# A hybrid attention and PEER layer on one core: one or two gathers used behind each of the last 20 tiles ahead of the first up product, and the second low part of these tiles on VectorE

## The chip, the core and the metric

The kernel runs on one core of a Trainium2 chip. Its engines are TensorE (PE, matmuls), VectorE (DVE), ScalarE (ACT), GpSimd (POOL) and SyncE (SP, which here only issues transfers); each works through its own row of instructions in order, and waits at an instruction until what it needs is there. Transfers run on 16 DMA engines. The metric is the time of one execution in microseconds (us) on the device, the median of several runs.

## What is computed

The reference is one layer: attention with two groups of heads, an output projection, and then PEER, a layer of 16,384 experts of one neuron each, of which every token chooses 128 (8 heads, 16 each). There are 512 tokens of width 2048, in float32. The change lies within PEER:

```
def peer(x, w_query, sub_keys, expert_down, expert_up):
    q = (xt @ w_query).reshape(T, PEER_HEADS, 2, PEER_HALF)
    scores = jnp.einsum('thpc,hpnc->thpn', q, sub_keys).astype(jnp.float32)
    vals, idx = lax.top_k(scores, PEER_TOPK)
...
    experts = (i1 * PEER_N_KEYS + i2).reshape(T, PEER_HEADS * PEER_TOPK)
    gates = jax.nn.softmax(top_vals, axis=-1)...
    def block(args):
        xc, ec, gc = args
        u = jnp.take(expert_down, ec, axis=0)
        hdn = jax.nn.gelu(jnp.einsum('ted,td->te', u, xc))
        vsel = jnp.take(expert_up, ec, axis=0)
        return jnp.einsum('te,ted->td', gc * hdn, vsel)
```

## The kernel before

PEER is computed in two ways at once. For the first 320 tokens the kernel multiplies with all experts: 128 **down tiles** (one for each 128 experts; 128 x 320 numbers come out, and GELU puts them into `hold`), a product with a dense table of gates, and **up products** that add into `yacc`. For the other 192 tokens it fetches only the chosen experts' rows: 384 **gather steps**. A step (`gather_step`) issues one indirect transfer on POOL's queue (128 rows of 2048 floats, one for each partition, into one of four buffers `rows`) and one **use** of them on DVE (L517 for the down table, which is a dot product, L525 for the up table, which adds into `yg`). The steps are part e (64 tokens twice, 64 steps down and 64 up), then part g (128 tokens, 128 and 128). At the end of part e its result is finished and written, and part g's row of inputs is loaded.

Matmuls are in a float32 form that takes two parts of each operand: `hi`, made by ACT from the loaded `raw`, and `lo`, the difference, made by DVE or POOL; three matmuls (L99 to L101) stand for one. A down tile consists of two pieces ("halves", 24 matmuls each); `down_tile(e, lo_on)` gives the engine that makes `lo` for each. There are two buffers of `hi` and two of `lo`, three of `raw`. An up product for one of 16 columns c has 24 matmuls and parts `uhi` and `ulo`, made by ACT and DVE from `uraw`.

The order in the program:
- the gates stage, in which the dense table of gates is made and written to memory (`o` comparisons on DVE, L680 and L681), with 40 gather steps;
- 38 down tiles ahead of the first up product: 28 whose `hold` is written to memory for later, and 10 that stay. I number them 0 to 37. Before the change POOL makes both low parts of tiles 0 to 27; of tiles 28 to 37 POOL makes the first and DVE the second, and one gather step stands behind each;
- the main loop, 16 groups g of 16 columns c. At the start of a group its eight `hold` are split into `hn` parts (L801 on ACT, L802 on DVE). For the first 180 columns there is one down tile (both low parts on DVE) for every two columns, for the last 76 there is none; `due` counts the gather steps behind each column.

A scheduler decides where on each engine the instructions stand, from the order of the program and its own costs; a gather step's use is only tied to stand behind the matmul that it was given. So several tiles of the 38 stand among the gates stage's instructions: the trace has tiles 19 to 37 behind it.

```
        for e in range(NE1 - SPILL, NE1):
            down_tile(e, (G, G))
            DMA.dma_start(hid_d[e - (NE1 - SPILL)], hold[e])
        for e in range(HOLD):
            mm = down_tile(e, (G, V))
            gather_step(mm)
```

## Time and profile before

| | |
|---|---|
| median of 3 runs | 3319.63 us (3317.11 to 3323.86) |
| profiled execution: its time, its span | 3313.15 us, 3311.4 us |
| TensorE busy | 3098.8 us, 94% of the span |
| DVE busy | 2497.5 us, 75% |
| POOL busy | 967.6 us, 29% |
| granted TensorE clock, mean | 0.976 of full speed |
| transfers | 846.50 MB, mean 256 GB/s |

The span runs from the first instruction to the last of the profiled execution. A share of busy time is a mean over stages with different limits: what a change in one stage is worth is read from that stage.

### The profile page before, as it was taken

The numbers are of one execution on the slowest core, as the hardware profiler recorded it, in microseconds if no ns is written. First come the engines' busy times: TensorE is split into PE (matmuls) and PEld (weight loads), VectorE is DVE, ScalarE is ACT, GpSimd is POOL, SyncE is SP. The second block draws the span as 40 slices with busy tenths as digits, with TensorE's granted clock in tenths as the row PEclk, the third lists the DMA queues.
The fourth block names the chain that finished last, engine by engine and source line by source line (L and its number), as shares of the span: only waits on it lengthen the run. The fifth ranks groups of instructions, "written<-read, shape, count | busy, mean of one in ns | idle before, by whom it ended". The sixth has DMA issues, their size and how long they took to land.

```text
span 3311.4 us, 47208 instructions
## 1 busy us (share of the span) xinstructions
PE 3098.8 (94%) x18265; PEld 2828.8 (85%) x18265; DVE 2497.5 (75%) x3724; ACT 1214.8 (37%) x1863; POOL 967.6 (29%) x529
## 2 busy tenths in 40 slices
PE   6999999999998877889999999999999999998987
PEld 4887778878876667778999999999999999998877
DVE  5225665454357899992799998998999999988885
ACT  4224444343231117884333333332333333322233
POOL 2000000000024445766434433333433344432210
PEclk9999999999999889999999999999999999999999
DMA  4322222214432136887799999999999999999983
GB/s 178 98 94 75 69 69 73 70 62 137 130 128 71 64 116 239 323 331 266 278 391 388 394 397 365 396 402 359 378 404 392 397 396 404 374 377 366 349 307 117
DMA packets 215792, 846.50 MB, mean 256 GB/s; under 512 B 20944, under 2 KB 69456, under 8 KB 163216
## 3 DMA queue, kind: packets, MB, share of 16 engines
q1 hardware_dynamic: 159424, 439.37, 37.1%
q0 software_dynamic: 55296, 402.68, 30.5%
q8 instruction: 143, 2.34, 0.3%
q10 hardware_dynamic: 848, 1.44, 0.1%
q14 instruction: 81, 0.66, 0.1%
HBM read 806.31 MB, written 35.91 MB: 254 GB/s over the span
## 4 chain that ended last, share of the span: by engine, by line
PE 42%; DVE 11%; issue 5%; DMA 3%; POOL 2%; ACT 0%; SPq 0%; ACTq 0%; DVEq 0%; POOLq 0%
PE up L99 7%; PE up L100 7%; PE up L101 7%; PE dn L99 7%; PE dn L100 7%; PE dn L101 6%; DVE o L680 2%; DMA uraw<-in_up_t 2%; DVE o L681 2%; DVE rows L517 2%; DVE ulo L810 1%; DVE yg_g L525 1%; POOL rows L511 1%; POOL lo L94 1%; DVE hn L802 1%
## 5 line engine op out<-in xcount | busy, mean ns | idle before, releaser
L93 ACT ACTIVATE hi<-raw 128x1024 fp32r<-128x1024 f32 x416 | 439.8, 1058 | 733.1 <-PE dn L101 221.9
L99 PE MATMUL up<-hn,ulo 128*128 128x320 f32 x2048 | 646.6, 316 | 55.6 <-DVE ulo L810 55.1
L99 PE MATMUL dn<-hn,lo 128*128 128x320 f32 x2048 | 650.3, 318 | 44.3 <-POOL lo L94 41.8
L94 DVE TENSOR_TENSOR lo<-raw,hi 128x1024 fp32r<-128x1024 f32 x320 | 390.1, 1226 | 352.9 <-ACT hi L93 351.9
L100 PE MATMUL dn<-hn,hi 128*128 128x320 f32 x2048 | 647.2, 316 | 0.0
L101 PE MATMUL dn<-hn,hi 128*128 128x320 f32 x2048 | 645.6, 315 | 0.0
L100 PE MATMUL up<-hn,uhi 128*128 128x320 f32 x2048 | 640.3, 313 | 0.9 <-DVE hn L802 0.9
L101 PE MATMUL up<-hn,uhi 128*128 128x320 f32 x2048 | 639.6, 312 | 0.0
L809 ACT ACTIVATE uhi<-uraw 128x1024 fp32r<-128x1024 f32 x256 | 271.7, 1061 | 648.8 <-PE up L101 504.5
L99 PEld LDWEIGHTS up<-hn,ulo 128*128 128x128 f32 x2048 | 390.9, 191 | 70.4 <-DVE ulo L810 66.0
L99 PEld LDWEIGHTS dn<-hn,lo 128*128 128x128 f32 x2048 | 388.9, 190 | 54.1 <-POOL lo L94 50.5
L100 PEld LDWEIGHTS up<-hn,uhi 128*128 128x128 f32 x2048 | 391.2, 191 | 1.2 <-DVE hn L802 1.2
L101 PEld LDWEIGHTS up<-hn,uhi 128*128 128x128 f32 x2048 | 390.9, 191 | 0.0
L100 PEld LDWEIGHTS dn<-hn,hi 128*128 128x128 f32 x2048 | 389.2, 190 | 0.0
L101 PEld LDWEIGHTS dn<-hn,hi 128*128 128x128 f32 x2048 | 388.8, 190 | 0.0
L810 DVE TENSOR_TENSOR ulo<-uraw,uhi 128x1024 fp32r<-128x1024 f32 x256 | 309.3, 1224 | 49.4 <-PE dn L99 28.6
L511 POOL DMA_INDIRECT rows<-in_up,gidx x128 | 222.9, 1741 | 401.9 <-DVE yg_g L525 380.1
L511 POOL DMA_INDIRECT rows<-in_down,gidx x128 | 209.5, 1637 | 379.1 <-DVE rows L517 347.2
L94 POOL TENSOR_TENSOR lo<-raw,hi 128x1024 fp32r<-128x1024 f32 x96 | 246.3, 2571 | 209.2 <-ACT hi L93 209.0
L525 DVE SCALAR_TENSOR_TENSOR yg_g<-rows,coef_g,yg_g 128x2048 f32<-128x2048 f32 x127 | 298.0, 2347 | 0.0
L517 DVE SCALAR_TENSOR_TENSOR rows<-rows,hng_g 128x2048 f32<-128x2048 f32 x128 | 290.7, 2286 | 3.9 <-DMA rows<-in_down,gidx 2.3
L99 PE MATMUL mm<-xn,lo 128*128 128x512 f32 x512 | 204.5, 399 | 0.0
(259 smaller groups left out, 5003.3 us busy)
## 6 DMA issues: line engine op xcount, KB each, us to landing
raw<-in_down_t SPq DMA_DIRECT2D x256, 512.0 KB
uraw<-in_up_t SPq DMA_DIRECT2D x256, 512.0 KB
raw<-in_w_qk SPq DMA_DIRECT2D x64, 512.0 KB
g_d<-stg SPq DMA_DIRECT2D x10, 2048.0 KB
gt<-g_d SPq DMA_DIRECT2D x32, 640.0 KB
raw<-in_w_v SPq DMA_DIRECT2D x32, 512.0 KB
raw<-in_w_o SPq DMA_DIRECT2D x32, 512.0 KB
raw<-in_w_pq SPq DMA_DIRECT2D x32, 512.0 KB
```

What stands on the lines that cost most here:

```text
L93: A.activation(hi, raw, AF.Copy)
L94: (lo_on or V).tensor_tensor(lo, raw, hi.bitcast(F32), ALU.subtract)
L99: PE.matmul(ps, a[1], b[0], start=first, stop=False)
L100: PE.matmul(ps, a[0], b[1], start=False, stop=False)
L101: return PE.matmul(ps, a[0], b[0], start=False, stop=last)
L511: ld = G.indirect_dma_start(out=rows, out_offset=None, in_=table, in_offset=bass.IndirectOffsetOnAxis(ap=ix[:, j:j + 1], axis=0))
L517: use = V.scalar_tensor_tensor(rows, rows, 1.0, hng[part], ALU.mult, ALU.mult, accum_out=dots[part][:, j:j + 1])
L525: use = V.scalar_tensor_tensor(yg[part], rows, coef[part][:, j:j + 1], yg[part], ALU.mult, ALU.add)
L680: V.tensor_tensor(o2, iob, col(i2t), ALU.is_equal)
L681: V.tensor_tensor(o1, iob, col(i1t), ALU.is_equal)
L809: A.activation(uh, raw, AF.Copy)
L810: V.tensor_tensor(ul, raw, uh.bitcast(F32), ALU.subtract)
```

## The change

Of the 38 tiles ahead of the first up product, the last 20 (numbers 18 to 37) now have their second low part made by DVE, and one gather step behind each, two behind every second one: 30 steps instead of 10. Tiles 28 to 37 had DVE's low part before, so ten low parts move from POOL to DVE. The main loop issues 1.5 steps for a column instead of 1.6 while there are down tiles, and 0.75 instead of 0.8 behind them, since 314 steps are left for it instead of 334.

```diff
+FREE = 18
...
-        for e in range(NE1 - SPILL, NE1):
-            down_tile(e, (G, G))
-            DMA.dma_start(hid_d[e - (NE1 - SPILL)], hold[e])
-        for e in range(HOLD):
-            mm = down_tile(e, (G, V))
-            gather_step(mm)
+        for n, e in enumerate((*range(NE1 - SPILL, NE1), *range(HOLD))):
+            mm = down_tile(e, (G, V if n >= FREE else G))
+            if e >= NE1 - SPILL:
+                DMA.dma_start(hid_d[e - (NE1 - SPILL)], hold[e])
+            for _ in range((n >= FREE) + (n >= FREE and n % 2)):
+                gather_step(mm)
...
-                due += 1.6 if e < NE1 - SPILL else 0.8
+                due += 1.5 if e < NE1 - SPILL else 0.75
                 while due >= 1:
                     gather_step(mm)
                     due -= 1
```

The new constant moves every later line number by one. DVE's row from the end of the gates stage on, before (L517 are uses, L810 is a low part of the first up products, L94 a low part of a down tile):

```order
L681 TENSOR_TENSOR o_10432<-iota_e,i1t 128x1024
L517 SCALAR_TENSOR_TENSOR rows_10428,dots_e<-rows_10428,hng_e 128x2048
L517 SCALAR_TENSOR_TENSOR rows_10455,dots_e<-rows_10455,hng_e 128x2048
L810 TENSOR_TENSOR ulo<-uraw,uhi 128x1024 x2
L94 TENSOR_TENSOR lo<-raw,hi 128x1024
L517 SCALAR_TENSOR_TENSOR rows_12328,dots_e<-rows_12328,hng_e 128x2048
L94 TENSOR_TENSOR lo<-raw,hi 128x1024
```

The same place with the change (L518 are uses, L95 low parts of down tiles, L811 of up products):

```order
L682 TENSOR_TENSOR o_10432<-iota_e,i1t 128x1024
L95 TENSOR_TENSOR lo<-raw,hi 128x1024
L518 SCALAR_TENSOR_TENSOR rows_10428,dots_e<-rows_10428,hng_e 128x2048
L518 SCALAR_TENSOR_TENSOR rows_10455,dots_e<-rows_10455,hng_e 128x2048
L518 SCALAR_TENSOR_TENSOR rows_11689,dots_e<-rows_11689,hng_e 128x2048
L95 TENSOR_TENSOR lo<-raw,hi 128x1024
L518 SCALAR_TENSOR_TENSOR rows_11756,dots_e<-rows_11756,hng_e 128x2048
L518 SCALAR_TENSOR_TENSOR rows_11759,dots_e<-rows_11759,hng_e 128x2048
L95 TENSOR_TENSOR lo<-raw,hi 128x1024
L518 SCALAR_TENSOR_TENSOR rows_11826,dots_e<-rows_11826,hng_e 128x2048
L811 TENSOR_TENSOR ulo<-uraw,uhi 128x1024
L95 TENSOR_TENSOR lo<-raw,hi 128x1024
```

DVE had nothing of tiles 19 to 27 before; now a low part of each stands there, with one or two uses ahead of it, and the first two `ulo` stand among the tiles 20 to 22.

DVE's row in tiles 28 to 37, before (L789 is the product with the gates, L802 a `hn`):

```order
L94 TENSOR_TENSOR lo<-raw,hi 128x1024
L789 TENSOR_TENSOR hold_12392<-hold_12392,gt_12925 128x320
L802 TENSOR_TENSOR hn_6789<-hold_12392,hn_6788 128x320
L517 SCALAR_TENSOR_TENSOR rows_12460,dots_e<-rows_12460,hng_e 128x2048
L94 TENSOR_TENSOR lo<-raw,hi 128x1024
```

With the change:

```order
L95 TENSOR_TENSOR lo<-raw,hi 128x1024
L790 TENSOR_TENSOR hold_12371<-hold_12371,gt_12988 128x320
L803 TENSOR_TENSOR hn_6789<-hold_12371,hn_6788 128x320
L518 SCALAR_TENSOR_TENSOR rows_12439,dots_e<-rows_12439,hng_e 128x2048
L518 SCALAR_TENSOR_TENSOR rows_12442,dots_e<-rows_12442,hng_e 128x2048
L95 TENSOR_TENSOR lo<-raw,hi 128x1024
L790 TENSOR_TENSOR hold_12437<-hold_12437,gt_12988 128x320
L803 TENSOR_TENSOR hn_6789<-hold_12437,hn_6788 128x320
L518 SCALAR_TENSOR_TENSOR rows_12508,dots_e<-rows_12508,hng_e 128x2048
L95 TENSOR_TENSOR lo<-raw,hi 128x1024
```

Every second tile has two uses between `hn` and the next tile's low part. POOL's row has, in all 20 tiles, one low part and then one or two transfers of `rows`.

DVE's row at the seam between groups 4 and 5 of the main loop, before (L817 adds an up product into `yacc`; the last but one and the last of group 4 are here):

```order
L517 SCALAR_TENSOR_TENSOR rows_18481,dots_g<-rows_18481,hng_g 128x2048
L817 TENSOR_TENSOR yacc<-yacc,up 128x320
L517 SCALAR_TENSOR_TENSOR rows_18580,dots_g<-rows_18580,hng_g 128x2048
L517 SCALAR_TENSOR_TENSOR rows_18583,dots_g<-rows_18583,hng_g 128x2048
L802 TENSOR_TENSOR hn_6789<-hold_17455,hn_6788 128x320
L802 TENSOR_TENSOR hn_6789<-hold_17611,hn_6788 128x320
L802 TENSOR_TENSOR hn_6789<-hold_17750,hn_6788 128x320
L802 TENSOR_TENSOR hn_6789<-hold_17887,hn_6788 128x320
L802 TENSOR_TENSOR hn_6789<-hold_18024,hn_6788 128x320
L802 TENSOR_TENSOR hn_6789<-hold_18161,hn_6788 128x320
L802 TENSOR_TENSOR hn_6789<-hold_18303,hn_6788 128x320
L810 TENSOR_TENSOR ulo<-uraw,uhi 128x1024 x2
```

With the change:

```order
L818 TENSOR_TENSOR yacc<-yacc,up 128x320
L803 TENSOR_TENSOR hn_6789<-hold_17497,hn_6788 128x320
L803 TENSOR_TENSOR hn_6789<-hold_17650,hn_6788 128x320
L803 TENSOR_TENSOR hn_6789<-hold_17789,hn_6788 128x320
L818 TENSOR_TENSOR yacc<-yacc,up 128x320
L518 SCALAR_TENSOR_TENSOR rows_18616,dots_g<-rows_18616,hng_g 128x2048
L518 SCALAR_TENSOR_TENSOR rows_18619,dots_g<-rows_18619,hng_g 128x2048
L803 TENSOR_TENSOR hn_6789<-hold_17926,hn_6788 128x320
L803 TENSOR_TENSOR hn_6789<-hold_18063,hn_6788 128x320
L803 TENSOR_TENSOR hn_6789<-hold_18200,hn_6788 128x320
L803 TENSOR_TENSOR hn_6789<-hold_18339,hn_6788 128x320
L811 TENSOR_TENSOR ulo<-uraw,uhi 128x1024 x2
```

Three of the seven `hn` stand ahead of the last `yacc` now. The seams of before differ in the number of uses behind the last `yacc` (one or two) and in how many `hn` stand ahead of it (none to three); with the change five seams are as this one, and six have one use behind the last `yacc`, with two `hn` and the other use between the last two `yacc` and five `hn` behind.

## Rows read from the trace of the kernel before

**Rows 1.** Windows: stretch, its length, busy us (instructions) by engine, granted clock, DMA share, GB/s.

```profile
1500.00:1550.00 50.00, 46.28 (x302) 44.34 (x303) 7.75 (x7) 21.72 (x31) 29.74 (x13) 1.00 0.89 300
1700.00:2000.00 300.00, 298.70 (x2021) 297.90 (x2020) 283.14 (x243) 104.62 (x130) 119.92 (x65) 1.00 1.00 392
2960.00:3200.00 240.00, 207.44 (x1304) 198.49 (x1304) 203.32 (x204) 66.23 (x79) 57.73 (x42) 0.94 0.93 346
```

**Rows 2.** Timeline of ACT, the `hold` of down tiles: start us, us, instruction, idle before.

```profile
1548.84 0.44 ACT L643 ACTIVATE hold<-dn 128x320 f32<-128x320 f32 x1 [3.08 <-PE dn L101]
1556.59 0.44 ACT L643 ACTIVATE hold<-dn 128x320 f32<-128x320 f32 x1 [3.08 <-PE dn L101]
...
1639.59 0.44 ACT L643 ACTIVATE hold<-dn 128x320 f32<-128x320 f32 x1 [2.24 <-PE dn L101]
1647.08 0.44 ACT L643 ACTIVATE hold<-dn 128x320 f32<-128x320 f32 x1 [2.22 <-PE dn L101]
...
1668.73 0.44 ACT L643 ACTIVATE hold<-dn 128x320 f32<-128x320 f32 x1 [2.50 <-PE dn L101]
1682.89 0.44 ACT L643 ACTIVATE hold<-dn 128x320 f32<-128x320 f32 x1 [2.50 <-PE dn L101]
...
2959.73 0.44 ACT L643 ACTIVATE hold<-dn 128x320 f32<-128x320 f32 x1 [6.06 <-PE dn L101]
```

**Rows 3.** The same view, at gaps longer than 14.16.

```profile
1996.19 0.44 ACT L643 ACTIVATE hold<-dn 128x320 f32<-128x320 f32 x1 [2.50 <-PE dn L101]
...
2050.71 0.44 ACT L643 ACTIVATE hold<-dn 128x320 f32<-128x320 f32 x1 [2.50 <-PE dn L101]
...
2121.51 0.44 ACT L643 ACTIVATE hold<-dn 128x320 f32<-128x320 f32 x1 [2.13 <-issue]
2136.59 0.44 ACT L643 ACTIVATE hold<-dn 128x320 f32<-128x320 f32 x1 [2.50 <-PE dn L101]
...
2235.70 0.44 ACT L643 ACTIVATE hold<-dn 128x320 f32<-128x320 f32 x1 [2.50 <-PE dn L101]
2253.86 0.44 ACT L643 ACTIVATE hold<-dn 128x320 f32<-128x320 f32 x1 [2.50 <-PE dn L101]
...
2310.50 0.44 ACT L643 ACTIVATE hold<-dn 128x320 f32<-128x320 f32 x1 [2.50 <-PE dn L101]
2329.25 0.44 ACT L643 ACTIVATE hold<-dn 128x320 f32<-128x320 f32 x1 [2.50 <-PE dn L101]
...
2699.90 0.44 ACT L643 ACTIVATE hold<-dn 128x320 f32<-128x320 f32 x1 [2.49 <-PE dn L101]
2714.45 0.44 ACT L643 ACTIVATE hold<-dn 128x320 f32<-128x320 f32 x1 [2.50 <-PE dn L101]
```

**Rows 4.** Timeline of DVE in tiles 29 and 30.

```profile
1588.39 1.23 DVE L94 TENSOR_TENSOR lo<-raw,hi 128x1024 fp32r<-128x1024 f32 x1 [3.68 <-ACT hi L93]
...
1592.43 2.42 DVE L802 TENSOR_TENSOR hn<-hold,hn 128x320 fp32r<-128x320 f32 x1 [2.41 <-ACT hn L801]
1594.77 2.28 DVE L517 SCALAR_TENSOR_TENSOR rows<-rows,hng_e 128x2048 f32<-128x2048 f32 x1
...
1596.98 1.22 DVE L94 TENSOR_TENSOR lo<-raw,hi 128x1024 fp32r<-128x1024 f32 x1
1598.12 0.48 DVE L789 TENSOR_TENSOR hold<-hold,gt 128x320 f32<-128x320 f32 x1
```

**Rows 5.** Timeline of DVE at the seam of groups 4 and 5.

```profile
2233.75 2.92 DVE L802 TENSOR_TENSOR hn<-hold,hn 128x320 fp32r<-128x320 f32 x7
```

**Rows 6.** Timelines of POOL and DVE in the gates stage.

```profile
1386.15 2.80 POOL L94 TENSOR_TENSOR lo<-raw,hi 128x1024 fp32r<-128x1024 f32 x1 [4.24 <-ACT hi L93]
...
1386.64 4.46 DVE L517 SCALAR_TENSOR_TENSOR rows<-rows,hng_e 128x2048 f32<-128x2048 f32 x1
```

**Rows 7.** Timeline of POOL, the first low part of tile 30.

```profile
1592.12 2.38 POOL L94 TENSOR_TENSOR lo<-raw,hi 128x1024 fp32r<-128x1024 f32 x1 [4.03 <-ACT hi L93]
```

**Rows 8.** DMA queues in the window 1505 to 1655: all transfers.

```profile
DMA packets 14430, 39.78 MB, mean 265 GB/s; under 512 B 1092, under 2 KB 7492, under 8 KB 12968
```

## The prediction

> **What bounds the kernel now.** I read the stretches first, then the gaps between tiles, then single instructions. Four stretches matter: the gates stage up to 1505 us; the last 20 tiles ahead of the first up product (1505 to 1655, "the free stretch"); the up products with a down tile for every two of them (1655 to 2960, "the paired stretch"); the up products alone (2960 to 3295). In the windows [rows 1] the reader is to see that DVE is nearly idle at the start of the free stretch (7.75 of 50 us), that TensorE is full in the paired stretch (298.7 of 300 us, granted clock 1.00) with DVE at 283.1 and the transfers at a share of 1.00 and 392 GB/s, and that in the last stretch neither is full (PE 207, DVE 203 of 240).
>
> The starts of `hold` on ScalarE give the time of every tile [rows 2]. A tile takes 7.75 us where POOL makes both low parts, 7.49 where DVE makes the second, and 14.16 with its two up products. The last is TensorE's own pace: 96 matmuls in 14.16 us, so half a tile (24 matmuls) is 3.54 us and a tile alone would be 7.08. From 1668.73 to 2959.73 there are 89 such gaps; 89 x 14.16 is 1260.2 of 1291.0 us. So the paired stretch loses 30.8 us in all, and only that can be won there, however much DVE work leaves it. Three gaps from 1996.19 to 2050.71 lose 12.0 (the end of part e), the one at 2310.50 loses 4.6 in the middle of a group, and ten of the eleven seams between groups share the other 14.2, and the eleventh lies within the end of part e [rows 3].
>
> **The main loop: 20 uses leave it.** A use costs DVE 2.21 us (1594.77 to 1596.98) [rows 4]. 288 uses in the paired stretch become 270: 18 x 2.21 is 40 us of DVE time, but its price is what TensorE stops waiting. At a seam TensorE has one down tile, 7.08 us, between the last product of a group and the first of the next, and in that time DVE must finish what stands between that product's `yacc` and the next `ulo`. Before, at the seam of 2235.70, these are two uses and seven `hn` (2.92 us in all [rows 5]): 0.4 for `yacc` (of the size of one `hn`), 4.4, 2.9 and 1.14 for `ulo` are 8.8, 1.7 too late, and the gap is 18.16, 4.0 lost, more than the lateness alone. The fractions of 1.6 repeat every five groups, so a second seam is like it. With 1.5 all seams are alike but for where three `hn` go: five have two uses and four `hn` there (0.4 + 4.4 + 1.7 + 1.14 = 7.6, half a us late), six have one use and five `hn` (0.4 + 2.2 + 2.1 + 1.14 = 5.8, in time). Before has one seam of each kind: 2121.51 lost 0.92, 2699.90 lost 0.39 [rows 3]. So 5 x 0.92 + 6 x 0.39 = 6.9 in place of the 14.2: **-7.3**. The lost 4.6 at 2310.50 came with four uses in front of a `ulo`; that order is gone from the middle of groups, but a late `raw` helped to make it: -4.6 at best, 0 at worst, **-2.5** taken. The end of part e issues the same instructions in the middle of a group: **0**, give or take 4. The paired stretch: **-10**, between -16 and -3.
>
> **The up products alone.** 46 uses become 44, so at most 2 x 2.21 = 4.4 us less DVE work where DVE often ends last; but the last use falls one product later, nearer to the closing work of part g: **-2**, between -4.4 and +3.
>
> **The free stretch: 20 uses and 10 low parts arrive.** DVE has the room by its busy time: a pair of tiles (one with one use, one with two) asks 3 x 2.21 + 2 x 1.14 = 8.9 us of 15. What speaks against it is that DVE and POOL don't work at once here. In the gates stage a use that met POOL's `lo` took 4.46 us instead of 2.28, and that `lo` took 2.80 instead of 2.38, since it began behind a running comparison [rows 6]. In the last ten tiles every `hn` takes 2.42 us behind a `lo` of 2.38 that began 0.31 earlier [rows 4, 7]. So to DVE's time POOL's `lo` must be added, and what counts is who comes first.
>
> Tiles 18 to 27. I count from the start of the second `lo` on DVE (1588.39), which takes 1.14; then the uses stand, the first from +1.1 to +3.35, the second to +5.56. POOL wants its `lo` for the next tile at +3.73 (1592.12). In a tile with one use DVE is done at +3.35 and nothing meets. In one with two, the second use starts 0.4 us ahead of POOL, which waits from 3.73 to 5.56, 1.83 us (that it waits behind a use I take from its wait behind a comparison, the nearest row), and TensorE, which in these tiles waits for that `lo` already, waits with it. A pair costs 7.49 + 7.49 + 1.83 = 16.8 us instead of 2 x 7.75 = 15.5: +1.3, five pairs, +6.5. Without that wait the ten tiles would gain 10 x 0.26 = 2.6, which is the lower bound.
>
> Tiles 28 to 37, counted from the end of POOL's `lo` (1594.50). Now `hn` ends at +0.27, a use at +2.48 and the second `lo` is ready at +3.6, just when TensorE has done its first half. With two uses `lo` starts at +4.69 and ends at +5.83; POOL's next `lo`, wanted at +5.12, stands behind it until 8.2. TensorE's second half runs from 5.83 to about 9.4, and an ordinary tile of 7.49 follows: 16.9 a pair instead of 14.98, +1.9, five pairs, **+9.5**. The lower bound is 0, if DVE catches up in the tile with one use. The free stretch: **+16**, between -3 and +24 (8 us of late transfers on top, next).
>
> The Trainium skill, "SBUF — State Buffer", section "Who interferes with whom", has a rule for this: a DVE instruction that reads two inputs from SBUF and a GpSimd instruction that reads SBUF exclude each other, and the one issued second waits for the whole of the first. That the use waits is in these traces (4.46 for 2.28); that POOL's `lo` waits behind a running use, which is the whole of the +6.5, no row shows, only the wait behind a comparison. By the rule it does, and the sum stands; by the shown rows alone the ten tiles could give 2.6 back and the sum would be 9 lower, -5.
>
> **Transfers.** A gather is 128 rows of 2048 floats, 1.05 MB. The free stretch moved 39.8 MB [rows 8]; 20 more make 60.8 MB in 150 us, 405 GB/s, more than the 392 at which the paired stretch is saturated. At 392 it needs 155 us, and about 5 more for its start, where a share of 0.89 moved only 300 GB/s [rows 1]. If the stretch becomes 166 us long by the port, the transfers fit, and hide; early lumps can make a `raw` or the first two `uraw` late, whose `ulo` now stand in DVE's row among the first tiles. No price in the sum, up to +8 in the range.
>
> **Sum.** On the profiled execution (span 3311.4, time 3313.15): +16 - 10 - 2 = **+4**. The median of the runs shown is 6.5 us above that execution, so I put the sum on the median: 3319.6 + 4 = **3323.6 us**. A measurement of this kernel can tell about 0.2%, 6.6 us, from no change; the forecast lies inside that.
>
> **Rivals.**
> 1. Faster: the exclusion costs little. DVE lies idle for stretches of each tile now, and if its row and POOL's `lo` slip past each other, tiles 18 to 27 give 2.6 and the others stay at 7.49; then -3 - 10 - 2 = -15, **3305 us**. For it: the port's own load in a pair of tiles 28 to 37 is 3 x 2.21 + 2 x (1.14 + 0.8 + 2.38) = 15.3 us (0.8 for `hn` and the gate product), hardly over 14.98. Against it: both rows are fixed orders with TensorE between them, and the walk above finds no other place for the second use. It decides where the ten pairs cost under 0.7 us each.
> 2. Slower: the port's +16 and the lumps of transfers at 1505 to 1540 together, with the paired stretch giving only its two bad seams: +22 - 6 + 0 = +16, **3336 us**. It decides where the free stretch grows beyond about 18 us; the 405 GB/s speak for it, the four `rows` buffers filled beforehand (4 x 1.05 MB, 10 us of transfers) against.
> 3. The moved work does nothing, since TensorE is at its pace in 14.16 either way and the free stretch has room: 0 to -3, **3318 us**. The seam of 2235.70 speaks against the first half.
>
> **Chances.** The forecast (+4, from -3 to +10) 0.37; rival 1 0.27; rival 2 0.26; rival 3 0.10. Faster by over 0.2%: rival 1 nearly whole, 0.27. Slower: rival 2 with the upper part of the forecast, 0.36. Within: 0.37. The range takes rival 1 from its middle and rival 2 to its middle: 3305 to 3336.
>
> **What would show it.** Right: tile gaps in the free stretch that alternate between about 7.5 and 9.3, with POOL's `lo` behind a use and DVE's `lo` behind two; seams of the paired stretch all at 14.5 to 15.1, no gap over 15.2 but for the end of part e, and a sum of losses of about 20 in place of 30.8. Wrong: gaps of 7.5 throughout the free stretch (rival 1), or gaps over 10 that end with a `raw`, a `uraw` or `rows` transfer (rival 2); or seams that still lose 4. The likeliest fault is the size of the wait at the port, since it hangs on 0.4 us between the second use and POOL's `lo`.

## The result, and the profile after

The change makes the kernel slower: 3340.47 us in the median (3333.16 to 3344.35) against 3318.37 (3315.39 to 3324.82) for the kernel before, run beside it; the ratio is 1.0063, 95% interval 1.0048 to 1.0077. The profiled execution took 3341.1 us with a span of 3339.3. That is 27.9 us over the profiled span of before, 5.8 more than the medians differ, since the execution profiled before lies below its median. The stages below are compared span against span, one profiled execution of each kernel.

Cut by the starts of `hold`, the 27.9 us arise in three places:

| stretch, by `hold` | before | after | difference | forecast |
|---|---|---|---|---|
| up to tile 18 | 1508.40 | 1508.38 | 0.0 | 0 |
| tiles 18 to 22 | 32.70 | 47.43 | +14.7 | |
| tiles 22 to 37 | 113.48 | 127.27 | +13.8 | |
| free stretch, both together | 146.18 | 174.70 | +28.5 | +16 |
| tile 37 to the last down tile | 1305.15 | 1295.82 | -9.3 | -10 |
| from there to the end | 351.67 | 360.40 | +8.7 | -2 |

Windows of the changed kernel, with columns as in [rows 1]; the last one starts 20 us later than there, since the stretch does:

```profile
1500.00:1550.00 50.00, 36.54 (x216) 35.23 (x215) 24.61 (x21) 16.86 (x26) 21.45 (x11) 0.86 0.95 348
...
1700.00:2000.00 300.00, 291.17 (x1935) 287.48 (x1934) 271.25 (x237) 101.93 (x126) 109.60 (x62) 0.98 0.99 376
2980.00:3220.00 240.00, 203.07 (x1265) 196.70 (x1263) 192.95 (x195) 63.50 (x76) 49.46 (x38) 0.92 0.89 324
```

In the first 50 us TensorE works 36.5 us where it worked 46.3, and the transfers carry 348 GB/s where they carried 300. In the last window DVE works 10 us less than before, the transfers are less full, and yet TensorE does less: something waits there that is neither engine's total.

**The hole behind tile 19.** ACT's timeline, from the `hold` of tile 19 to that of tile 20 and on:

```profile
1516.65 0.44 ACT L644 ACTIVATE hold<-dn 128x320 f32<-128x320 f32 x1 [2.45 <-PE dn L102]
1521.13 1.06 ACT L94 ACTIVATE hi<-raw 128x1024 fp32r<-128x1024 f32 x1 [4.04 <-DMA raw<-in_down_t]
1523.64 1.06 ACT L94 ACTIVATE hi<-raw 128x1024 fp32r<-128x1024 f32 x1 [1.46 <-DMA raw<-in_down_t]
1538.32 1.06 ACT L810 ACTIVATE uhi<-uraw 128x1024 fp32r<-128x1024 f32 x1 [13.62 <-DMA uraw<-in_up_t]
1539.28 0.42 ACT L644 ACTIVATE hold<-dn 128x320 f32<-128x320 f32 x1
1539.60 1.99 ACT L94 ACTIVATE hi<-raw 128x1024 fp32r<-128x1024 f32 x2
```

From one `hold` to the next are 22.63 us (9.40 before). Both `raw` of tile 20 came late, and then ACT stood 13.62 us in front of a `uhi` whose `uraw` was not there, with the `hold` and the next tile's two `hi` behind it. SP's queue at that time, and the windows:

```profile
1517.12 0.57 SPq L775 DMA_DIRECT2D hid_d<-hold  x1
1517.78 9.22 SPq L788 DMA_DIRECT2D gt<-g_d  x2
1527.06 3.64 SPq L807 DMA_DIRECT2D uraw<-in_up_t  x1
1530.81 0.84 SPq L83 DMA_DIRECT2D raw<-in_down_t  x2
```

```profile
1510.00:1520.00 10.00, 9.89 (x67) 9.62 (x66) 6.63 (x5) 1.50 (x2) 5.53 (x4) 1.00 0.99 384
1520.00:1530.00 10.00, 7.08 (x37) 6.81 (x37) 3.44 (x3) 2.11 (x2) 4.93 (x3) 0.83 1.03 377
1530.00:1540.00 10.00, 2.40 (x17) 2.13 (x15) 0.59 (x1) 1.68 (x3) 0.00 (x0) 0.87 0.90 324
1540.00:1550.00 10.00, 8.04 (x37) 8.04 (x38) 6.80 (x6) 4.03 (x5) 4.64 (x3) 0.61 0.86 295
```

Two readings offer themselves. By **order**, the scheduler has put two `gt` and a `uraw` ahead of the `raw` (before, a `raw` stood between any two of these), and `uhi` ahead of `hold`. By **traffic**, the DMA engines are full (share 1.03) and the gathers that POOL now issues take their part: from 1500 to 1540 us these are the queues (packets, MB, share of the engines' time), SP's first and the gathers second:

```profile
q1 hardware_dynamic: 4262, 8.02, 55.8%
q0 software_dynamic: 891, 6.41, 40.6%
```

The gathers of before in the same time, and its window from 1510 to 1520:

```profile
q0 software_dynamic: 288, 2.10, 17.4%
```

```profile
1510.00:1520.00 10.00, 9.97 (x65) 9.35 (x63) 0.00 (x0) 2.56 (x3) 5.33 (x3) 1.00 0.97 370
```

The clock adds to it: after the idle stretch TensorE was granted 0.61 of full speed from 1540 to 1550 (1.00 before). From 1541.96 to 1547.72 its matmuls start about every 0.27 us in place of 0.15, so some 2.5 us of the 14.7 go to the lower level of the clock, an estimate from these rows.

**The pairs.** From tile 22 to 33, gaps alternate as foretold: 7.52 and 9.27 behind tiles 24 and 25, 7.12 and 10.59 behind tiles 30 and 31. DVE's two uses, and POOL's low part:

```profile
1591.91 2.28 DVE L518 SCALAR_TENSOR_TENSOR rows<-rows,hng_e 128x2048 f32<-128x2048 f32 x1
...
1594.12 2.28 DVE L518 SCALAR_TENSOR_TENSOR rows<-rows,hng_e 128x2048 f32<-128x2048 f32 x1
```

```profile
1594.50 4.12 POOL L95 TENSOR_TENSOR lo<-raw,hi 128x1024 fp32r<-128x1024 f32 x1 [4.04 <-ACT hi L94]
```

POOL's `lo` began 0.38 us behind the start of the second use and took 4.12 instead of 2.38: the whole of what was left of the use (to 1596.33, 1.83 us), and then its own time.

**The paired stretch.** Every seam is at 15.1 or 14.5:

```profile
2266.54 0.44 ACT L644 ACTIVATE hold<-dn 128x320 f32<-128x320 f32 x1 [2.50 <-PE dn L102]
2281.61 0.44 ACT L644 ACTIVATE hold<-dn 128x320 f32<-128x320 f32 x1 [2.50 <-PE dn L102]
...
2836.52 0.44 ACT L644 ACTIVATE hold<-dn 128x320 f32<-128x320 f32 x1 [2.50 <-PE dn L102]
2851.07 0.44 ACT L644 ACTIVATE hold<-dn 128x320 f32<-128x320 f32 x1 [2.50 <-PE dn L102]
```

Ten seams lose 6.0 us where they lost 14.1, and the stall of 4.6 at 2310.50 of [rows 3] is gone; the end of part e, with the eleventh seam, loses 16.1 in place of 12.0.

**The up products alone.** DVE at the start of group 12:

```profile
3037.22 2.35 DVE L811 TENSOR_TENSOR ulo<-uraw,uhi 128x1024 fp32r<-128x1024 f32 x2
3039.49 1.28 DVE L790 TENSOR_TENSOR hold<-hold,gt 128x320 f32<-128x320 f32 x3
3042.88 0.89 DVE L790 TENSOR_TENSOR hold<-hold,gt 128x320 f32<-128x320 f32 x2 [2.11 <-DMA hold<-hid_d]
3043.70 0.48 DVE L803 TENSOR_TENSOR hn<-hold,hn 128x320 fp32r<-128x320 f32 x1
3044.23 0.49 DVE L818 TENSOR_TENSOR yacc<-yacc,up 128x320 f32<-128x320 f32 x1
...
3048.81 1.30 DVE L790 TENSOR_TENSOR hold<-hold,gt 128x320 f32<-128x320 f32 x3 [2.21 <-DMA gt<-g_d]
...
3052.29 0.48 DVE L818 TENSOR_TENSOR yacc<-yacc,up 128x320 f32<-128x320 f32 x1
```

Five gate products on reloaded `hold` stand ahead of the first `yacc`, and DVE waits in them for the reload; three more stand ahead of the second, and it waits for a `gt`. So the first two `yacc` come 9.4 and 8.1 us behind the one ahead of them; before, 2.7 and 4.0, since its products stand further back there (where they cost most of that again, at columns 8 and 9). Group 13 begins alike, with 11.2 and 8.3; there before had 12.6 and 1.5, its last three products standing three `yacc` later. Counted by `yacc`, the change falls 2.5 us behind in the whole of group 12, 4.2 in group 13 (5.3 in its first two `yacc`, of which it wins a part back), and 2.4 in the last two groups.

### The profile page after: what moved, and what is told of

It is laid out like the page before. It is cut to its first block, busy times and chain, and to the rows that moved or that the text cites. A ratio compares the mean times of both kernels' runs of the same rounds, so it can differ in the third digit from the quotient of the medians.

```text
span 3339.3 us, 47159 instructions
## 1 busy us (share of the span) xinstructions
PE 3100.5 (93%) x18265; PEld 2833.2 (85%) x18265; DVE 2512.9 (75%) x3734; ACT 1214.5 (36%) x1863; POOL 952.8 (29%) x519
## 4 chain that ended last, share of the span: by engine, by line
PE 43%; DVE 11%; DMA 4%; issue 4%; POOL 1%; ACT 0%; SPq 0%; ACTq 0%; DVEq 0%; POOLq 0%
PE up L100 8%; PE up L101 8%; PE up L102 8%; PE dn L100 6%; PE dn L101 6%; PE dn L102 6%; DVE o L681 2%; DVE rows L518 1%; DVE o L682 1%; DMA raw<-in_down_t 1%; DVE yg_g L526 1%; DVE ulo L811 1%; DMA uraw<-in_up_t 1%; DVE hn L803 1%; DMA hold<-hid_d 1%
## 5 line engine op out<-in xcount | busy, mean ns | idle before, releaser
L94 ACT ACTIVATE hi<-raw 128x1024 fp32r<-128x1024 f32 x416 | 439.8, 1058 | 757.5 <-PE dn L102 238.4
L95 DVE TENSOR_TENSOR lo<-raw,hi 128x1024 fp32r<-128x1024 f32 x330 | 403.4, 1225 | 344.6 <-ACT hi L94 343.2
L810 ACT ACTIVATE uhi<-uraw 128x1024 fp32r<-128x1024 f32 x256 | 271.5, 1061 | 651.4 <-PE up L102 575.5
L512 POOL DMA_INDIRECT rows<-in_down,gidx x128 | 241.0, 1883 | 383.8 <-DVE rows L518 343.1
L512 POOL DMA_INDIRECT rows<-in_up,gidx x128 | 200.6, 1567 | 466.4 <-DVE yg_g L526 450.2
L811 DVE TENSOR_TENSOR ulo<-uraw,uhi 128x1024 fp32r<-128x1024 f32 x256 | 310.6, 1218 | 30.7 <-ACT uhi L810 30.6
L518 DVE SCALAR_TENSOR_TENSOR rows<-rows,hng_g 128x2048 f32<-128x2048 f32 x128 | 289.4, 2285 | 9.1 <-DMA rows<-in_down,gidx 6.3
L95 POOL TENSOR_TENSOR lo<-raw,hi 128x1024 fp32r<-128x1024 f32 x86 | 229.7, 2676 | 203.4 <-ACT hi L94 203.2
```

The costliest lines, as they stand in the source:

```text
L94: A.activation(hi, raw, AF.Copy)
L95: (lo_on or V).tensor_tensor(lo, raw, hi.bitcast(F32), ALU.subtract)
L512: ld = G.indirect_dma_start(out=rows, out_offset=None, in_=table, in_offset=bass.IndirectOffsetOnAxis(ap=ix[:, j:j + 1], axis=0))
L518: use = V.scalar_tensor_tensor(rows, rows, 1.0, hng[part], ALU.mult, ALU.mult, accum_out=dots[part][:, j:j + 1])
L810: A.activation(uh, raw, AF.Copy)
L811: V.tensor_tensor(ul, raw, uh.bitcast(F32), ALU.subtract)
```

## The experiments

Their stages, by `hold` as above; "last" is from the last down tile to the end of the span. The ratio is to the kernel before, run beside each; the row of before is the one beside the change. Each stage is read from one execution, and places that an edit leaves as they were differ by some us: the `hold` of tile 18 starts between 1506.2 and 1511.2 in the fourteen kernels, and the last stretch of before and of runs 1 and 11, with the same steps, is 349.0 to 351.7.

| kernel | 18 to 22 | 22 to 37 | paired | last | median us | ratio (95%) |
|---|---|---|---|---|---|---|
| before | 32.7 | 113.5 | 1305.2 | 351.7 | 3318.4 | |
| the change | 47.4 | 127.3 | 1295.8 | 360.4 | 3340.5 | 1.0063 (1.0048 to 1.0077) |
| 1 low parts alone | 30.7 | 112.4 | 1306.0 | 349.0 | 3310.4 | 0.9980 (0.9968 to 0.9992) |
| 2 steps alone | 43.9 | 133.6 | 1292.7 | 363.3 | 3342.3 | 1.0080 (1.0067 to 1.0093) |
| 3 no low part on POOL | 46.9 | 117.8 | 1294.8 | 358.6 | 3330.1 | 1.0045 (1.0029 to 1.0061) |
| 4 first loads held back | 34.0 | 137.0 | 1294.6 | 357.9 | 3337.2 | 1.0065 (1.0052 to 1.0079) |
| 5 0.8 at the end | 47.0 | 126.2 | 1294.6 | 347.2 | 3324.2 | 1.0023 (1.0012 to 1.0034) |
| 6 uses, no transfers | 34.8 | 121.9 | 1296.9 | 357.0 | 3323.3 | 1.0027 (1.0015 to 1.0039) |
| 7 transfers, no uses | 44.6 | 123.0 | 1293.6 | 363.2 | 3333.1 | 1.0048 (1.0030 to 1.0066) |
| 8 as 3, uses apart | 44.3 | 112.2 | 1296.8 | 360.7 | 3322.1 | 1.0021 (1.0008 to 1.0035) |
| 9 steps from tile 22 | 30.7 | 126.2 | 1308.3 | 352.9 | 3327.3 | 1.0024 (1.0004 to 1.0045) |
| 10 as 9, uses apart, no POOL | 33.0 | 111.0 | 1303.6 | 350.7 | 3311.8 | 0.9985 (0.9973 to 0.9997) |
| 11 as before, no POOL | 32.4 | 106.8 | 1302.5 | 351.3 | 3302.2 | 0.9965 (0.9952 to 0.9977) |
| 12 as 11, steps at the end | 32.0 | 106.8 | 1297.1 | 375.6 | 3324.4 | 1.0021 (1.0006 to 1.0036) |

The theories: **port and row** (uses and low parts of DVE and POOL keep each other waiting), **order** and **traffic** as above.

**1. The low parts alone.** Against the change:

```diff
-            for _ in range((n >= FREE) + (n >= FREE and n % 2)):
+            for _ in range(1 if e < HOLD else 0):
...
-                due += 1.5 if e < NE1 - SPILL else 0.75
+                due += 1.6 if e < NE1 - SPILL else 0.8
```

> Ten low parts of tiles 18 to 27 move to DVE, but the gather steps stay as before (one behind each of tiles 28 to 37, 1.6 and 0.8 a column). Port theory (the lengthened tiles come from DVE's second use and POOL's low part keeping each other out): no use stands among these ten tiles, so each takes 7.49 in place of 7.75 and the free stretch is 2.6 us shorter than before, tiles 28 to 37 as before; time 0 to 4 us below before, ratio 0.999. Order theory (the hole of 13 us behind tile 19 comes from where the first uraw loads and the first uhi stand in their rows): two raw stand between the gt loads and the first uraw here, so no hole. Rival, that a DVE low part in these tiles is itself what lengthens them: the free stretch 15 us longer, ratio 1.005.

The free stretch is 143.1 us, 3.1 below before, and the time 0.2% below (7.4 us, more than the 0 to 4 that I gave). This half of the change is a small gain; DVE's low part lengthens nothing. So the change's loss comes with its steps: added to this run, they take the free stretch from 143.1 to 174.7.

**2. The steps alone.**

```diff
-            mm = down_tile(e, (G, V if n >= FREE else G))
+            mm = down_tile(e, (G, V if e < HOLD else G))
```

> The 30 gather steps of the change, but POOL makes both low parts of tiles 18 to 27 as before. Port theory: in these tiles a pair now has four low parts of 2.38 on POOL and three uses of 2.21 on DVE that can't overlap, 16.2 us where before took 15.5 and the change about 16.6, so the ten tiles stay within 3 us of the change and tiles 28 to 37 are as in the change. Rival, that DVE's row alone (its low part behind two uses) lengthens tiles 18 to 27: they go back to 7.75 each, 15.5 a pair. Order theory for the hole behind tile 19: one raw stands ahead of the first uraw here and the other behind it, so the hole is smaller than in the change, 3 to 9 us in place of 13. Traffic theory (the added gathers fill the DMA engines, whatever the order): the hole stays at 13. Time: 3331 to 3342 by order, 3338 to 3344 by traffic.

The time does not tell the theories apart. The gap behind tile 19 is 12.3, about as order had foretold, but the three others up to tile 22 are 9.8, 11.8 and 10.1: the loss up to tile 22 is 11.2 where the change has 14.7, spread over four tiles. Order sets where the loss shows more than how much it is. POOL's two low parts make the tiles behind slower still (133.6), more than I had allowed.

**3. No low part on POOL.**

```diff
-            mm = down_tile(e, (G, V if n >= FREE else G))
+            mm = down_tile(e, (V, V) if n >= FREE else (G, G))
```

> The change, with both low parts of tiles 18 to 37 on DVE, so that POOL does nothing there but issue gathers; the same transfers in nearly the same order. Port theory: with no low part on POOL nothing excludes; DVE's own load for a pair of tiles is 3 x 2.21 + 4 x 1.14 + 4 x 0.45 = 13.0 us, below TensorE's 14.16, so tiles 20 to 37 take 7.1 to 7.5 each, 123 to 129 us for the 17 gaps in place of 143.8. Traffic theory (61 MB in that stretch is more than the engines carry): the gaps stay at 8.2 to 8.5 on average. For the hole, two more raw stand ahead of the first uraw here than in the change: order theory says under 5 us, traffic theory 13. Time by port and order 3308 to 3322, by traffic 3335 to 3341.

Tiles 22 to 37 fall by 9.5 us, to 117.8, which the port asks for, but are still 4.3 over before; the 17 gaps took 135.9, above the 129 that I had set as the upper end, and the time of 3330.1 lies between what I gave for the two theories. The gap behind tile 19 is still 21.6, 12.2 over before, although two more `raw` stand ahead of the first `uraw`: the order theory had said under 5, the traffic theory 13. POOL makes no low part here, so its issuing of gathers ahead of a `lo` is not what makes the hole either. What is left in the pairs is DVE's own row: two uses in one piece, with both low parts behind them.

```profile
1606.50 2.28 DVE L518 SCALAR_TENSOR_TENSOR rows<-rows,hng_e 128x2048 f32<-128x2048 f32 x1
...
1608.71 2.29 DVE L518 SCALAR_TENSOR_TENSOR rows<-rows,hng_e 128x2048 f32<-128x2048 f32 x1
...
1610.92 2.35 DVE L95 TENSOR_TENSOR lo<-raw,hi 128x1024 fp32r<-128x1024 f32 x2
```

**4. The first loads held back.**

```diff
+                    if e1 < 8:
+                        tc.add_manual_dep(ld.ins, tmm[22 + e1 // 2], PACE, reason="late")
...
+                if g == 0 and c < 3:
+                    tc.add_manual_dep(ld.ins, tmm[30 + 2 * c], PACE, reason="late")
```

> The change, with the first gt loads held back in SP's row until behind tiles 22 and 24, and the first three uraw loads until behind tiles 30, 32 and 34 (so their uhi and ulo too). Nothing else of the work changes. Order theory: the gap behind tile 19 falls from 22.6 to 9 or 10 us, the other gaps stay as they are, and the time falls by 12 to 14 us against the change, to 3326 to 3329. Traffic theory: the hole stays, or comes back where the loads now stand, and the time stays within 4 us of the change's 3340.5.

The hole goes from its place (9.53) and comes back where the loads now stand: tiles 22 to 37 take 9.7 us more, its free stretch is 171.0 against 174.7, and the time of 3337.2 is the one that traffic had foretold. ACT there:

```profile
1612.31 0.44 ACT L644 ACTIVATE hold<-dn 128x320 f32<-128x320 f32 x1 [0.81 <-PE dn L102]
1620.09 1.06 ACT L816 ACTIVATE uhi<-uraw 128x1024 fp32r<-128x1024 f32 x1 [6.39 <-DMA uraw<-in_up_t]
1622.36 0.41 ACT L644 ACTIVATE hold<-dn 128x320 f32<-128x320 f32 x1
```

Order says where the transfers' lateness falls, not whether it does.

**5. 0.8 in place of 0.75 at the end.**

```diff
-                due += 1.5 if e < NE1 - SPILL else 0.75
+                due += 1.5 if e < NE1 - SPILL else 0.8
```

> The change with 0.8 steps for each of the last 76 columns in place of 0.75 (as before the change), so that the steps end about four columns earlier; the 1.5 and the free stretch stay. In the change DVE's row has, at the starts of groups 12, 13 and 14, five gate products on reloaded hold ahead of the first yacc of the group; with 0.8 group 12 has none there. Theory of the row's order (the 8.7 us that the last stretch lost come from that one start): the last stretch falls from 360.4 to 349 to 353 us, the time by 8 to 11 to about 3331. Rival (the stretch lost because it has to catch up on transfers, whatever the order): within 3 us of 360, time 3338 to 3342.

The last stretch falls by 13.2 us to 347.2, a little under what I had set, the time by more than the 8 to 11 (13 by the ratios), and the places are not quite mine. At the start of group 12 no gate product stands ahead of the first two `yacc`, and DVE doesn't wait for loads:

```profile
3036.46 1.22 DVE L811 TENSOR_TENSOR ulo<-uraw,uhi 128x1024 fp32r<-128x1024 f32 x1
3037.60 0.48 DVE L818 TENSOR_TENSOR yacc<-yacc,up 128x320 f32<-128x320 f32 x1
3038.00 2.35 DVE L526 SCALAR_TENSOR_TENSOR yg_g<-rows,coef_g,yg_g 128x2048 f32<-128x2048 f32 x1
```

But what that wins is lost again at columns 7 to 9, where the products now stand, and group 12 ends no earlier than in the change. Group 13 begins with 12.2 and 1.5 in place of 11.2 and 8.3, as before; by group 14 the run is 5.3 us ahead of the change. The other 8 come at the start of group 15, 3.1 us in place of 11.6: part g ends earlier, and its closing work no longer stands in that seam. Before lost there too (12.0), so this part is a gain over before and not a loss of the change undone. The row's order it is, but at groups 13 and 15 rather than at 12.

**6. The uses without 20 of the transfers; 7. the transfers without 20 of the uses.** Both keep one transfer, or use, behind each of tiles 28 to 37 as before. In the one a step loads nothing and its use reads `hng` twice; in the other

```diff
+        if not (work or last):
+            use = V.tensor_copy(dots[part][:, j:j + 1], rows[:, 0:1])
...
-            for _ in range((n >= FREE) + (n >= FREE and n % 2)):
-                gather_step(mm)
+            for k in range((n >= FREE) + (n >= FREE and n % 2)):
+                gather_step(mm, e < HOLD and k == 0)
```

> The change with 20 of its 30 transfers of the free stretch left out (all of tiles 18 to 27, every second one of a pair in 28 to 37), their uses kept at the same length on DVE (they read the row of inputs twice in place of the fetched rows, so the sums are others). Traffic theory of the hole behind tile 19: it goes, the gap of 22.6 becomes 9 or 10. Order theory: it stays over 16. Theory of the rows (DVE's and POOL's, for the lengthened pairs): the 17 gaps from tile 20 to 37 stay at 140 to 148 us as in the change (143.8). If transfers lengthened these, they fall to 129 to 134. Traffic for the hole and rows for the pairs give a free stretch of about 161 in place of 174.7 and 3326 to 3329.

> The other half: all 30 transfers of the free stretch as in the change, but the uses of 20 of them left out on DVE but for a copy of one column (so the sums are others). Traffic theory of the hole: it stays, 18 to 24 us where the change has 22.6. Theory of the rows for the pairs: the 17 gaps from tile 20 to 37 fall to 127 to 133 us, since no pair has two uses now. If transfers lengthened the pairs, they stay at 138 or more. Traffic for the hole and rows for the pairs: free stretch about 158, time 3322 to 3328.

The two take the change's loss apart; their times, 3323.3 and 3333.1, lie under and over what I gave. Up to tile 22 the uses alone lose 2.1 us and the transfers alone 11.9, of 14.7 together. Windows with the uses alone, then with the transfers alone:

```profile
1520.00:1530.00 10.00, 8.00 (x44) 7.73 (x43) 7.12 (x7) 2.44 (x3) 4.28 (x1) 0.83 0.70 215
1530.00:1540.00 10.00, 9.90 (x67) 9.64 (x66) 3.58 (x4) 4.45 (x5) 2.67 (x2) 1.00 0.88 295
```

```profile
1520.00:1530.00 10.00, 8.32 (x46) 8.32 (x47) 2.52 (x3) 2.81 (x4) 3.33 (x2) 0.83 1.06 398
1530.00:1540.00 10.00, 4.15 (x29) 3.88 (x27) 0.60 (x1) 1.69 (x2) 0.00 (x0) 0.83 1.01 377
```

TensorE's hole of 1530 to 1540 stands where DVE works 0.60 us, and not where it works 3.58: it is the transfers'. My expectation for it was one gap; with the transfers alone it is three of 11.8 to 13.2. From tile 22 to 37 the uses alone lose 8.4 us (the 17 gaps from tile 20 took 140.3, in my range), the transfers alone 9.5 (148.0, where the row theory had said 127 to 133, so there it failed), both together 13.8. A late `raw` shows there, with the transfers alone, and later a `lo` of POOL that the one use of its tile, from 1621.21 to 1623.42, has lengthened (2.38 otherwise):

```profile
1589.08 1.06 ACT L94 ACTIVATE hi<-raw 128x1024 fp32r<-128x1024 f32 x1 [3.94 <-DMA raw<-in_down_t]
```

```profile
1621.80 3.91 POOL L95 TENSOR_TENSOR lo<-raw,hi 128x1024 fp32r<-128x1024 f32 x1 [4.52 <-ACT hi L94]
```

**8. As 3, with the two uses apart.** `down_tile` issues the first step of a pair behind its first half (the whole step, so its transfer moves along with its use):

```diff
+            if mid and piece == 0:
+                gather_step(mm)
```

> Both low parts of tiles 18 to 37 on DVE (so POOL has none), and in each tile with two steps one is tied to its first half and one to its second, so that a low part stands between two uses in DVE's row. With both low parts on DVE but the two uses together, the 17 gaps from tile 20 on took 135.9 us, in pairs of 7.12 and about 8.9. If what was left there is the two uses in one piece ahead of a low part, they fall to 122 to 127 us and the time by 9 to 13 to about 3320; if it is transfers (that stretch moved 352 GB/s), they stay at 132 to 138 and the time at 3326 to 3332. The hole behind tile 19 stays by the traffic theory, 18 to 24 us.

From tile 22 on, 112.2 us with all 30 uses and transfers, 1.2 below before: 12 of 15 gaps are 7.1 to 7.3, TensorE's own. DVE there, one use between any two low parts:

```profile
1582.03 1.23 DVE L95 TENSOR_TENSOR lo<-raw,hi 128x1024 fp32r<-128x1024 f32 x1 [0.56 <-ACT hi L94]
1583.17 2.28 DVE L518 SCALAR_TENSOR_TENSOR rows<-rows,hng_e 128x2048 f32<-128x2048 f32 x1
...
1585.92 1.23 DVE L95 TENSOR_TENSOR lo<-raw,hi 128x1024 fp32r<-128x1024 f32 x1 [0.46 <-ACT hi L94]
```

The 17 gaps sum to 133.1, in the range that I had given to transfers, but only since the hole reaches past tile 20 (11.9 and 8.9 behind it); it is still there, 11.6 in all up to tile 22, though the gap behind tile 19 is 16.3 and not 18 to 24.

**9. The steps from tile 22 on; 10. the same with the uses apart and no low part on POOL.** Both with 0.8 at the end; 9 is

```diff
-            for _ in range((n >= FREE) + (n >= FREE and n % 2)):
+            for _ in range((n >= 22) + (n >= 22 and n % 2)):
```

> The change with the gather steps starting behind tile 22 in place of 18 (24 in place of 30 in the free stretch), and 0.8 in place of 0.75 at the end; the low parts as in the change. Traffic theory of the hole: tiles 18 to 22 took 47.4 us in the change, 32.7 before, 34.8 with the uses alone and 44.6 with the transfers alone; with no new gather there they go back to 31 to 34. The pairs behind them keep both their prices: 22 to 37 at 122 to 130 (change 127.3, before 113.5). The last stretch 347 to 351 as in the run with 0.8. Time about 3340 - 15 - 2 - 11 = 3312, 3308 to 3318. If the hole comes from something else in the change, tiles 18 to 22 stay over 40 and the time over 3322.

> As the run with steps from tile 22 on, but with both low parts of tiles 18 to 37 on DVE and, in tiles with two steps, one tied to each half. If port, two uses in one piece and the early transfers are all that the free stretch lost, nothing of it is left: tiles 18 to 22 at 29 to 33, 22 to 37 at 107 to 114 (the split run had 112.2 with one gap of 11.5 in it), paired stretch 1293 to 1297, last stretch 347 to 351: a time of 3292 to 3302, faster than both kernels. If the transfers still cost 9 us in tiles 22 to 37 (as with the transfers alone), 117 to 124 there and 3303 to 3312.

With no new gather there, the hole is gone (30.7 and 33.0), while the pairs keep their price in 9 (126.2) and lose it in 10 (111.0). In the free stretch both came as expected. Both times are over what I gave, and the place is one that I had left out: the end of part e loses 24.0 and 23.1 us (12.0 before, 16.1 with the change, and 19.0 in run 1, whose steps are those of before), and the paired stretch is 1308 and 1304 in place of 1295.

**11. No low part on POOL, and the steps as before the change.**

```diff
-            mm = down_tile(e, (G, V if n >= FREE else G))
+            mm = down_tile(e, (V, V) if n >= FREE else (G, G))
...
-            for _ in range((n >= FREE) + (n >= FREE and n % 2)):
+            for _ in range(1 if e < HOLD else 0):
...
-                due += 1.5 if e < NE1 - SPILL else 0.75
+                due += 1.6 if e < NE1 - SPILL else 0.8
```

> The steps as before the change (ten, 1.6 and 0.8 a column), with both low parts of tiles 18 to 37 on DVE. It takes the port away with no new transfer and no new use: with the second low part alone on DVE tiles 22 to 37 took 112.4 us. Port theory: a tile falls from 7.5 to TensorE's 7.1, 106 to 109 us there, and the time to 3303 to 3309. If the 7.5 are POOL's or DVE's latency and not the port, 111 to 113 and 3308 to 3313. Paired stretch 1303 to 1307 and last stretch 348 to 352 as before in both cases.

Tiles 22 to 37 take 106.8 us, 7.12 each, TensorE's pace:

```profile
1621.28 0.44 ACT L644 ACTIVATE hold<-dn 128x320 f32<-128x320 f32 x1 [2.14 <-PE dn L102]
1628.40 0.44 ACT L644 ACTIVATE hold<-dn 128x320 f32<-128x320 f32 x1 [2.14 <-PE dn L102]
```

At 3302.2 us it is the fastest of all, 0.35% below before and about 1% below the change by the ratios. That this is the port is not shown. In run 1 tiles 23 to 25 take 7.48 each, with DVE at no work while POOL makes its `lo`, which takes its own 2.37:

```profile
1557.39 2.37 POOL L95 TENSOR_TENSOR lo<-raw,hi 128x1024 fp32r<-128x1024 f32 x1 [5.11 <-ACT hi L94]
```

DVE makes the same `lo` in 1.23, and that is enough to bring such a tile to 7.12. My expectation had given latency as a rival, but as if it stayed where it was; these runs leave it as the nearer cause, and the port untested here.

**12. The 18 steps at the end instead.** As 11, with `due += 1.5 if e < NE1 - SPILL else 1.0`.

> Ten steps in the free stretch and both low parts of tiles 18 to 37 on DVE, as in the run that has taken 3302 us, with 1.5 steps a column in place of 1.6 in the paired stretch and 1.0 in place of 0.8 behind it, so that the 18 steps go to the end instead of to the free stretch. Theory of the seams: the paired stretch falls from 1302.5 to 1293 to 1297 us with every seam at 14.5 to 15.1, whatever the free stretch does; the free stretch stays at 137 to 141. In the last stretch DVE gets 18 x 2.21 = 40 us more work than with 0.8: where it ends last there that shows, +10 to +30 over 351, and the time is 3304 to 3325. If the last stretch has DVE time to spare, within 4 us of 351 and a time of 3292 to 3300.

The paired stretch falls to 1297.1 with every seam at 14.5 to 15.1 but for the end of part e, and the last stretch grows by 24.3 over run 11. Its window has DVE at 218.9 of 235 us and TensorE at 203.8:

```profile
2985.00:3220.00 235.00, 203.81 (x1242) 191.15 (x1240) 218.87 (x207) 66.75 (x83) 77.56 (x51) 0.94 0.97 376
```

What the seams give comes without any change to the free stretch; but the steps have no free place at the end either.

## Why the prediction was wrong

The sign that I gave the sum was right, its size not: +4 us in place of +27.9 (22.1 by the medians), and the time lies 4.5 us over the range. Of the 23.9 us between the two, 12.5 are the free stretch's, 10.7 the last stretch's and 0.7 the paired stretch's.

**The step that failed** is "If the stretch becomes 166 us long by the port, the transfers fit, and hide ... No price in the sum, up to +8 in the range." I divided the whole stretch's bytes by its whole length. But the gathers come at its start, where before already moved 370 GB/s at a share of 0.97 (1510 to 1520), with the last store of the gates and the first `gt`, and where the first `uraw` follows. From 1500 to 1540 the gathers moved 6.4 MB in place of 2.1; the 4.3 more are 11 us at the 384 GB/s that the change had from 1510 to 1520, an estimate from these numbers. The transfers alone cost 11.9 us up to tile 22 (run 7), and with no new gather ahead of tile 22 that loss was gone (run 9). The same new transfers further on cost less: with the uses apart and no low part on POOL, tiles 22 to 37 took 111.0 us with 24 steps (run 10) and 106.8 with ten (run 11). I had named these lumps in rival 2, with 0.26, but had given them 6 us on top of a paired stretch that gives little; the lumps came, with 14.7 up to tile 22, while the paired stretch gave what I had said, so that its 3336 is the nearest of the four times is in part luck. The Trainium skill, "DMA: Bandwidth & Descriptors", section "Queues, rings and completion order", says that a DMA engine takes its queues in turn; in the trace the gathers took 40.6% of the engines' time and SP's loads 55.8%. That both were served side by side agrees, though no row shows the turns. So a gather that nobody waits for yet holds back a `raw` or a `uraw` that TensorE waits for.

**The second step** that failed is the last stretch, "-2, between -4.4 and +3". I counted uses, and they did go: DVE works less there. But 0.75 in place of 0.8 gave DVE's row another order at the starts of groups 12 and 13, with products ahead of `yacc` that wait for loads: +8.7. Taking back that number alone (run 5) took 13.2 off, more than was lost; about 6 of it are at group 13, nothing at group 12, and 8 at group 15, where before lost as well. The order is fixed and could have been read beforehand; I had looked at the seams of the paired stretch only.

**The pairs** came about in size, and the waits of my walk are in the trace, but I had called the whole +16 the port's. Tiles 22 to 37 lost 13.8, against the +16 for all 20. A pair of tiles 22 to 25 took 16.8 us, as forecast; that of 26 and 27 took 18.3, since behind its wait for POOL's `lo` TensorE was granted 0.77 of full speed from 1600 to 1605; one of 28 to 33 took 17.4 to 17.7, in place of 16.9; tiles 34 to 36 lost almost nothing. That POOL's `lo` waits behind a running use, which I had taken from the wait behind a comparison, is now shown (4.12 us at 1594.50), and it agrees with the rule of the Trainium skill, "SBUF — State Buffer", section "Who interferes with whom".

Taking POOL's low parts away gives 9.5 us back in tiles 22 to 37 (run 3), setting the uses apart 5.5 more (run 8). But 6.7 of the 9.5 come without any new step too (113.5 to 106.8, run 11). What the 20 new steps cost there is 14.9 us with the low parts of the change (from run 1, 112.4, to 127.3), 11.0 with none on POOL (from run 11, 106.8, to run 3, 117.8), and 5.4 with the uses apart as well (run 8, 112.2). So only about 4 of the 14.9 go with POOL's low parts; most of it is there with DVE's row and the transfers alone. With none on POOL, DVE has one low part more behind the two uses, so these runs don't divide the price exactly.

The transfers alone lose 9.5 there too (run 7). Late `raw` as such are not enough for that: between 1554 and 1655 ACT waited 10.2 us for `raw` in run 7 and 24.6 in run 8, where most gaps are TensorE's own. In run 7 POOL's `lo` took 3.41, 3.91 and 3.90 us in three tiles, behind the one use that was left, so the port is in it as well; how much each is worth stays open, and the two losses overlap (8.4 and 9.5 alone, 13.8 together). One term the walk left out: issuing a gather occupies POOL, 1.62 us on average in the change's free stretch (25 issues) and 1.09 before (10 issues). No run shows what that costs.

**The paired stretch** came near what I had worked out, -9.3 for -10. I had set 6.9 for eleven seams against 14.2 of ten; the ten lose 6.0. The stall of 2310.50 is gone whole (-4.6, where I took -2.5), but it is absent in run 1 too, with the spacing of before, so that 1.5 removed it is not shown. The end of part e is +4.1, at the edge of "0, give or take 4". That it was 12 to 24 us over the runs shows that I had no theory of that place; what sets it stays open.

Rival 1 (faster) fell with the pairs, rival 3 with them too: moved work was neither free where it went nor worthless where it left.

## What to carry to other kernels

Bytes over a long stretch say little: compare a new transfer with what the queues carry in the ten microseconds in which it will be issued, and start it where the share is low. Work that moves into idle time of an engine with its row in order costs what stands behind it, so place it between two things that others wait for, never two pieces together, and look whether another engine is shut out meanwhile. A constant that only spreads work also decides an order; read the new order at every seam, not only at those that one means to mend. And take a change of two halves apart: here the low parts alone gained 0.2%, and the steps lost 28 to 30 us, with the low parts of the change (run 1 to the change) as with none on POOL (run 11 to run 3).

## What the runs showed of the hardware that I had not expected

Full DMA engines did not slow TensorE by themselves, here as in the paired stretch of before [rows 1]. Windows of run 8, then of the change:

```profile
1560.00:1640.00 80.00, 77.56 (x513) 76.61 (x512) 62.93 (x63) 27.90 (x39) 19.43 (x16) 0.99 0.99 376
```

```profile
1560.00:1640.00 80.00, 72.12 (x460) 69.44 (x459) 50.60 (x44) 24.36 (x31) 50.60 (x24) 0.98 0.86 318
```

At a share of 0.99 TensorE is busy 77.6 of 80 us, at 0.86 only 72.1. And SP's queue itself can stand: two `gt` issues took 9.22 us at 1517.78 (0.60 and 8.58), when the engines' share was 1.03, and the `uraw` and `raw` behind them were issued that much later. A full share alone does not do it: before, the same two took 0.38 and 0.43, the second with the share at 1.00 (1520 to 1530). Why it stood is not shown.
